# Probabilities times values in the first two mixers: from split operands to whole 32-bit operands, two heads in the column halves of the array

## The chip, the cores and the metric

One core of one Trainium2 chip runs the whole program once. The metric is the device time of that execution in microseconds (us). Engines are named as the profile names them: PE is TensorE's matrix multiply, PEld its weight load, DVE is VectorE, ACT is ScalarE, POOL is GpSimd, SP issues most of the DMAs.

## The reference

A residual stream of 512 tokens by 1024 features passes through two blocks, all in 32-bit floats. The first block has two layers, each a mixer and a squared-ReLU MLP; the mixers are the part that the change touches. A mixer holds 16 attention heads of width 64. In layer 0 these are 8 heads with a forget gate and 8 with a relative position bias; in layer 1 they are 8 heads of stick-breaking attention and 8 of latent attention (MLA). For every head the end is the same product over 512 queries and the keys that they may see:

```
p = softmax(scores + bias)            # or, in layer 1, the stick-breaking weights a
out = einsum('bhqk,bkhd->bqhd', p, v) # 64 values per head
...
x = x + concat(heads) @ w_out
x = x + squared_relu_mlp(rmsnorm(x), w_up, w_down)
```

The second block (differential attention, sparse attention, gates, SwiGLU) follows; the change does not edit its code.

## The kernel before, in words

Activations lie with features along the 128 partitions and the 512 tokens along the free axis. PE is fed with a short 32-bit format (fp32r in the rows). To keep the precision of whole 32-bit numbers each operand is split into two short parts, hi and lo, with hi + lo the number: ACT copies hi, DVE subtracts hi from the source to get lo (`split`), and products are sums of matmuls over the parts. Weight blocks are split in the same way as they arrive (`wr` raw, `wh` and `wl` the parts).

All instructions are first recorded by a `Recorder`, then issued engine by engine in the order of a list schedule (`schedule`), which uses planned durations (`cost`) and numbers of buffers (`BUFS`). So every instruction has the same line in the trace, L371, and rows are told apart by the names of their tiles.

A pair of heads t has heads u = 0 and 1. The steps that the change touches, for one head:

- `softmax` makes four probability tiles (names `x`), one per 128 queries, with the scores in `pss`; `turn` transposes them on PE (`psp<-cst,x`) into four tiles by keys j, `pt0` to `pt3`, 512, 384, 256 and 128 queries wide, and splits each: ACT writes hi (`pt<-psp`), DVE lo (`pt<-psp,pt`). In `stick_head` there is no transposition; an exponential in a tile `P` is masked and then split by POOL (hi, `pt<-P`) and DVE (lo, `pt<-P,pt`). Its first split, of another quantity, uses a `pt0` tile for j = 0 too.
- `v_tiles` makes the value tiles `V`, per head 64 columns hi beside 64 columns lo, with an ACT and a DVE instruction per 128 tokens.
- `av` multiplies. The stationary operand is the 128 columns (hi, lo) of V of one head, the moving one is hi, then lo of `pt`, so eight matmuls of all 128 columns of the array into the one buffer `pso`: rows 0:64 hold hi of V, rows 64:128 lo.
- `fold` adds the two halves of `pso` (ACT copies one to a `T` tile, DVE adds) into half u of a tile; `finish_pair` splits that tile for the output projection.

There are 16 pairs (32 heads, 8 of them stick-breaking). While PE waits for one head, the schedule puts matmuls of projections in between (`psg` and, in `fill`, parts of the output projection). Buffers: three `psg`, two `pss`, two `psp`, one `pso`; one tile of each `pt0` to `pt3`.

One more place matters, in the second block: `compress` multiplies whole 32-bit operands, with 62 stationary columns.

```
for l in range(16):
    ...
    nc.tensor.matmul(ps[0:62, 0:256], win[l // 8][:, l % 8].rearrange("p g c -> p (g c)"),
                     wt[:, 256 * (l % 2):256 * (l % 2) + 256], start=(l == 0), stop=(l == 15))
```

Its weight tile `wt` is named `rbcq` or `acc` in turn and serves two of the 16 matmuls; the stationary tile is `strip`.

Of the kernel before, what the change touches and what calls it, by code (L numbers as in the profile page):

```python
# [20 lines left out]
NT = 4  # L21
# [14 lines left out]
# --------------------------------------------------------------------------  # L36
# host side: layouts only
# --------------------------------------------------------------------------
class Packer:
    """Weights as one flat array of contiguous [128, width] blocks."""  # L40
# [12 lines left out]
    def stationary(self, key, w, cols=None):  # L53
        """[128 K, 128 M] pieces in the order (m, kt), eight to a block."""
# [31 lines left out]
class Columns:  # L86
    """Small [128, n] arrays side by side."""
# [161 lines left out]
class Recorder:  # L249
# [14 lines left out]
    def later(self, k):  # L264
        """what is recorded inside yields to the next k instructions, but for those that wait for it"""
# [4 lines left out]
    def flush(self):  # L270
        """all that is recorded so far comes first"""
# [49 lines left out]
    def cost(self, op):  # L321
# [7 lines left out]
        if e == "tensor":  # L329
# [3 lines left out]
            if op.args[2].dtype == F32:  # L333
                return max(4 * n / 2.4, 428)
# [19 lines left out]
    # from the end of one instruction to the start of a dependent one on another engine  # L354
# [26 lines left out]
    def sequence(self):  # L381
        """the instructions by priority: each before those that wait for it, what comes later in its own order"""
# [116 lines left out]
# --------------------------------------------------------------------------  # L499
# chip side  # L500
# --------------------------------------------------------------------------
class Net:
# [21 lines left out]
    def fetch(self, m, tag="x"):  # L524
        """residual tile m on chip"""
# [13 lines left out]
    def c(self, key):  # L539
# [4 lines left out]
            "sm": 16, "sm32": 3, "rbc": 1, "rbcq": 1, "strip": 2}  # L544
# [28 lines left out]
    def split(self, dst, src, scale=None):  # L573
        """dst[:, 0] + dst[:, 1] = src (* scale per partition), two short parts."""
# [19 lines left out]
    def gemm(self, key, mov, evac, tags="gggggggg", cols=slice(0, 512), kept=None):  # L594
        """out[m] = W[:, m]^T mov; evac(m, psum)."""
# [17 lines left out]
    def gemm_tok(self, key, stat, evac, blk=None):  # L613
        """out[token tile i] = stat^T W; evac(i, psum)."""
# [33 lines left out]
    def mean_cols(self, acc, n, eps=None):  # L648
        """[128 tokens, tiles] mean of squares (+ eps)."""
# [19 lines left out]
    def rows(self, col, outs):  # L669
        """[128, 512] with col[token] in every row; outs = [(tag, factor)]."""  # L670
# [12 lines left out]
    def prep(self, m, gain, spill=False, sq=0):  # L683
        """operand x*g of feature tile m and its share of the sum of squares."""
# [29 lines left out]
    def to_stack(self, ab):  # L714
        """per head [hi; lo]"""
# [8 lines left out]
    def to_dup(self, ab):  # L724
        """per head a tile (hi, lo) with its rows twice"""
# [18 lines left out]
    def softmax(self, i, passes, bias, gate=None):  # L744
        """P [128 q, keys] from negated scores, normalised."""
# [14 lines left out]
    def turn(self, ps_list):  # L760
        """four P tiles -> per key tile j [128 keys, (hi, lo), q]"""
        nc = self.nc
        res = []
        for j in range(NT):
# [4 lines left out]
            t = self.tl(f"pt{j}", [128, 2, w], F32R)  # L769
            self.split(t, pp[:, :w])  # L770
            res.append(t)
        return res

# [7 lines left out]
    def fold(self, o, dst, u):  # L781
        """O = rows 0:64 + rows 64:128, into half u of dst"""
# [5 lines left out]
    def v_tiles(self, key, stat, rcol, extra=None, blk=None):  # L788
        """value tiles [128 tokens, 4 heads, (hi, lo), 64]"""
# [3 lines left out]
        def evac(i, ps):  # L793
            t = self.tl("V", [128, 4, 2, 64], F32R)
# [24 lines left out]
    def soft_head(self, passes, bias, v, dst, u, gate=None):  # L819
        ps_list = [self.softmax(i, passes, bias, gate) for i in range(NT)]  # L820
        pt = self.turn(ps_list)
        o = self.psum("o")
        self.av(o, pt, v)
        self.fold(o, dst, u)
# [20 lines left out]
    def out_part(self, key, ops):  # L845
        """first part of an output projection, one residual tile at a time"""
# [14 lines left out]
    def even_mixer(self):  # L861
# [9 lines left out]
        vt = self.v_tiles("fox_v0", h, self.rcol, gates, self.first)  # L871
# [10 lines left out]
        # sums within a token tile, and of the tiles one, two and three before  # L882
# [32 lines left out]
        for kind, mk in (("fox", fox_bias), ("chk", chk_bias)):  # L915
            for t in range(4):
                if not (kind == "fox" and t == 0) and t % 2 == 0:
                    vt = self.v_tiles(f"{kind}_v{t // 2}", h, self.rcol)
# [16 lines left out]
    def odd_mixer(self):  # L935
# [10 lines left out]
        for t in range(4):  # L946
            if t % 2 == 0:
                vt = self.v_tiles(f"sb_v{t // 2}", h, self.rcol)
# [818 lines left out]
```

## Time and profile before

| What | Value |
|---|---|
| Median of 3 runs | 2093.58 us (2093.03 to 2095.36) |
| Profiled execution, span from first to last instruction | 2093.9 us |
| Mean granted TensorE clock of that execution | 0.991 |
| PE, PEld busy | 2038.8 us (97%), 1688.3 us (81%) |
| DVE, ACT, POOL busy | 1131.0, 896.5, 399.1 us (54%, 43%, 19%) |

The profiled execution is another one than the three timed; its span is 0.3 us above their median. Busy shares are means over a program with different stages; matmuls are pipelined, so that the busy time of PE contains overlaps, and the distance from the start of one matmul to the start of the next says more than the duration in its row. The first mixer runs from about 40 to 240 us of the span, the second from about 655 to 905 us; an MLP follows each, and the second block fills the time after some 1250 us.

### The profile page before, as it was taken

How to read it: one execution, taken by the hardware profiler on the slowest of the kernel's cores; microseconds unless marked ns; L12 is line 12 of the kernel's file. 1: busy time of each engine (PE TensorE's matmuls, PEld its weight loads, DVE VectorE, ACT ScalarE, POOL GpSimd, SP SyncE). 2: the span in 40 equal slices, each digit the busy share in tenths (PEclk: the TensorE clock that was granted, in tenths of full speed). 3: DMA queues.
4: the chain of work that ended last, by engine and by line, in shares of the span. 5: the costliest groups of instructions: out<-in, count | busy, mean ns of one | idle time of the engine just before them, and what ended most of it. 6: DMA issues, size and time to landing. Idle time of an engine off the chain costs nothing. (4 is left out here: it accounts for less than half of the span.)

```text
span 2093.9 us, 27228 instructions
## 1 busy us (share of the span) xinstructions
PE 2038.8 (97%) x9958; PEld 1688.3 (81%) x9958; DVE 1131.0 (54%) x2033; ACT 896.5 (43%) x1621; POOL 399.1 (19%) x524
## 2 busy tenths in 40 slices
PE   8999999999999999899999999989999999999998
PEld 7887878888888877778888888877788888888887
DVE  5657853443445666774434344766786644333334
ACT  5556542322335555643323243544685542222224
POOL 2343210000022453220000014212240221011013
PEclk9999999999999999999999999999999999999999
DMA  6445623323244415632333234474113222223222
GB/s 197 133 129 157 186 91 92 100 91 101 91 142 122 111 58 129 181 104 91 100 92 98 94 120 131 126 185 126 57 41 111 92 100 91 101 91 101 90 101 81
DMA packets 80294, 232.00 MB, mean 111 GB/s; under 512 B 11424, under 2 KB 15392, under 8 KB 80160
## 3 DMA queue, kind: packets, MB, share of 16 engines
q1 hardware_dynamic: 80160, 230.25, 35.9%
q8 instruction: 79, 1.29, 0.3%
q14 instruction: 55, 0.45, 0.1%
HBM read 183.04 MB, written 10.49 MB: 92 GB/s over the span
## 5 line engine op out<-in xcount | busy, mean ns | idle before, releaser
L371 PE MATMUL psg<-h,wh 128*128 128x512 f32 x2688 | 855.4, 396 | 0.9 <-ACT h L371 0.6
L371 ACT ACTIVATE wh<-wr 128x1024 fp32r<-128x1024 f32 (+3 forms) x313 | 326.6, 1043 | 864.3 <-PE psg L371 687.4
L371 PEld LDWEIGHTS psg<-h,wh 128*128 128x128 f32 x2688 | 504.3, 189 | 108.2 <-ACT h L371 1.4
L371 PE MATMUL psg<-h,wl 128*128 128x512 f32 x1344 | 532.5, 396 | 1.0 <-DVE wl L371 0.7
L371 DVE TENSOR_TENSOR wl<-wr,wh 128x1024 fp32r<-128x1024 f32 (+3 forms) x313 | 385.0, 1230 | 58.8 <-ACT wh L371 54.8
L371 PEld LDWEIGHTS psg<-h,wl 128*128 128x128 f32 x1344 | 253.9, 189 | 56.6 <-DVE wl L371 2.7
L371 PE MATMUL psg<-KK,wh 128*128 128x512 f32 (+1 forms) x788 | 240.6, 387 | 0.4 <-DVE V L371 0.2
L371 DVE TENSOR_TENSOR x<-psg,x 128x512 f32<-128x512 f32 (+1 forms) x120 | 78.2, 654 | 290.8 <-PE psg L371 290.7
L371 POOL TENSOR_TENSOR acc<-acc,T 128x512 f32<-128x512 f32 (+1 forms) x50 | 73.5, 1471 | 789.6 <-issue 639.5
L371 PE MATMUL psg<-V,wh 128*128 128x512 f32 (+1 forms) x672 | 207.9, 390 | 1.0 <-DVE G L371 1.0
L371 PEld LDWEIGHTS psg<-KK,wh 128*128 128x128 f32 x788 | 146.6, 188 | 32.2 <-ACT o L371 0.5
L371 PE MATMUL psg<-KK,wl 128*128 128x512 f32 (+1 forms) x394 | 151.7, 385 | 0.0
L371 PEld LDWEIGHTS psg<-V,wh 128*128 128x128 f32 x672 | 126.2, 189 | 29.0 <-ACT wh L371 1.1
L371 DVE SCALAR_TENSOR_TENSOR T<-psg,rbc 128x512 f32<-128x512 f32 x64 | 44.3, 692 | 174.9 <-PE psg L371 172.6
L371 PE MATMUL psg<-V,wl 128*128 128x512 f32 (+1 forms) x336 | 131.6, 392 | 0.0
L371 ACT ACTIVATE x<-x,sm 128x128 f32<-128x128 f32 (+1 forms) x192 | 106.6, 558 | 52.5 <-DVE sm L371 52.0
L371 PE MATMUL psg<-o,wh 128*128 128x512 f32 x384 | 127.7, 401 | 0.8 <-ACT wh L371 0.5
L371 PE MATMUL psg<-wh,h 128*128 128x256 f32 (+2 forms) x560 | 114.2, 291 | 6.7 <-ACT wh L371 6.7
L371 PE MATMUL pso<-pt,V 128*128 128x128 f32 (+3 forms) x432 | 108.0, 337 | 3.5 <-ACT pt L371 1.9
L371 POOL TENSOR_SCALAR x<-x,sm 128x128 f32<-128x128 f32 (+1 forms) x112 | 66.5, 599 | 173.2 <-DVE sm L371 121.0
L371 PEld LDWEIGHTS psg<-wh,h 128*128 128x128 f32 x560 | 92.0, 193 | 8.4 <-ACT wh L371 6.7
L371 POOL TENSOR_TENSOR T<-T,rbc 128x512 f32<-128x512 f32 x22 | 39.3, 1785 | 285.3 <-ACT T L371 285.3
(263 smaller groups left out, 2673.8 us busy)
## 6 DMA issues: line engine op xcount, KB each, us to landing
wr<-in_w_dram SPq DMA_DIRECT2D x302, 512.0 KB, 3.5
KK<-AB SPq DMA_DIRECT2D x48, 256.0 KB, 5.4
QS<-AB SPq DMA_DIRECT2D x48, 128.0 KB, 3.9
x<-xs SPq DMA_DIRECT2D x24, 256.0 KB, 3.3
xs<-P SPq DMA_DIRECT2D x16, 256.0 KB, 3.8
xs<-x SPq DMA_DIRECT2D x16, 256.0 KB, 2.0
h<-AB SPq DMA_DIRECT2D x16, 256.0 KB, 3.8
KK<-AB SPq DMA_DIRECT2D x32, 128.0 KB, 2.4
```

Of the source, the lines that this page charges most:

```text
L371: op.inst = getattr(getattr(nc, op.eng), op.name)(*op.args, **op.kw)
```

## The change

The product of probabilities and values takes whole 32-bit operands in the 16 pairs. P is copied once (ACT) or used as it comes from the exponential (stick-breaking), V is written once; the DVE and POOL instructions of these splits go. One pair's two heads write one `pso` tile: head 0 rows 0:64, head 1 rows 64:128, with a stationary operand of 64 columns each, and `av_two` issues the two heads' matmuls of each j one after the other. `fold` is not called in the mixers, and `finish_pair` splits `pso` itself. `pt0` to `pt3` get two buffers, of half the width in bytes. The planner's cost of a 32-bit matmul with 64 output rows becomes half of what it was for others. The second block keeps the split form (`turn`, `av`, `fold`), with its two parts in two tiles.

```diff
-                return max(4 * n / 2.4, 428)
+                return 2 * n / 2.4 if out.ap[0][1] == 64 else max(4 * n / 2.4, 428)
...
-            "sm": 16, "sm32": 3, "rbc": 1, "rbcq": 1, "strip": 2}
+            "sm": 16, "sm32": 3, "rbc": 1, "rbcq": 1, "strip": 2, "pt0": 2, "pt1": 2, "pt2": 2, "pt3": 2}
...
+    def turn_whole(self, ps_list):
...
+            t = self.tl(f"pt{j}", [128, w])
+            nc.scalar.activation(t, pp[:, :w], AF.Copy)
+            res.append(t)
+        return res
+
+    def av_two(self, pts, vt, u0):
...
+        o = self.psum("o")
+        for j in range(NT):
+            for u in range(2):
+                nc.tensor.matmul(o[64 * u:64 * u + 64, 128 * j:], vt[j][:, u0 + u], pts[u][j], start=(j == 0), stop=(j == NT - 1))
+        return self.finish_pair(o)
...
+            if whole:
+                t = self.tl("V", [128, 4, 64])
+                nc.scalar.activation(t, ps[:, 0:256].rearrange("p (h d) -> p h d", h=4), AF.Copy, scale=rcol[:, i:i + 1])
+                res.append(t)
...
-                ob = self.T()
+                pts = []
                 for u in range(2):
                     passes = [(qs[:, u], kk[u][:, 0]), (qs[:, u], kk[u][:, 1])]
-                    self.soft_head(passes, mk(2 * t + u), self.vhead(vt, 2 * (t % 2) + u), ob, u)
-                ops.append(self.finish_pair(ob))
+                    pts.append(self.soft_head(passes, mk(2 * t + u)))
+                ops.append(self.av_two(pts, vt, 2 * (t % 2)))
...
             if j == 0:
-                sp[0] = self.pair("pt0")
+                sp[0] = self.halves("P")
...
-            e = self.tl("P", [128, 512])[:, :w]
+            e = at[j] = self.tl(f"pt{j}", [128, w])
             nc.scalar.activation(e, y[:, :w], AF.Exp)
...
-            a_ = self.tl(f"pt{j}", [128, 2, w], F32R)
-            nc.gpsimd.tensor_scalar(a_[:, 0], e, 1.0, 1.0, ALU.mult, ALU.mult)
-            nc.vector.tensor_tensor(a_[:, 1], e, a_[:, 0].bitcast(F32), ALU.subtract)
-            at[j] = a_
-        o = self.psum("o")
-        self.av(o, at, v)
-        self.fold(o, dst, u)
```

The order on PE shows where the new matmuls stand. First PE's order before, in the first mixer, at the second head of the first pair (`psg` is a projection, `psp` a transposition, `pso` the product; the last number is the width):

```order
L371 MATMUL pso_195<-pt_116_188,V_111 128x512
L371 MATMUL psg_285<-h_95,wh_287 128x512 x2
L371 MATMUL psg_285<-h_95,wl_288 128x512
L371 MATMUL psp_191<-cst,x_180 128x128
L371 MATMUL psp_191<-cst,x_184 128x128
L371 MATMUL pso_195<-pt_116_188,V_111 128x512
L371 MATMUL psp_193<-cst,x_184 128x128
L371 MATMUL pso_195<-pt_118_190,V_113 128x384 x2
L371 MATMUL psg_285<-h_97,wh_287 128x512
L371 MATMUL pso_195<-pt_120_192,V_115 128x256
```

Every row fills all 128 columns of the array; the products of one head are strewn among transpositions and projections. Now PE's order after the change, at the same pair: first the place of head 0's widest product, some 50 rows ahead of the rest.

```order
L371 MATMUL psp_162<-cst,x_151 128x128
L371 MATMUL psp_162<-cst,x_155 128x128
L371 MATMUL pso_192<-pt_87_159,V_111 64x512
L371 MATMUL psp_164<-cst,x_155 128x128
L371 MATMUL psg_269<-wl_268,h_95 128x256
```

This product of 64 columns stands alone between matmuls of 128 columns. Then the rest of the pair on PE, after the change:

```order
L371 MATMUL psp_188<-cst,x_181 128x128
L371 MATMUL pso_192<-pt_113_185,V_111 64x512
L371 MATMUL psp_190<-cst,x_181 128x128
L371 MATMUL pso_192<-pt_89_161,V_113 64x384
L371 MATMUL pso_192<-pt_115_187,V_113 64x384
L371 MATMUL pso_192<-pt_91_163,V_115 64x256
L371 MATMUL pso_192<-pt_117_189,V_115 64x256
L371 MATMUL pso_192<-pt_93_165,V_117 64x128
L371 MATMUL pss_223<-KK_207,QS_206 128x512
L371 MATMUL pso_192<-pt_119_191,V_117 64x128
L371 MATMUL pss_223<-KK_207,QS_206 128x512
```

Head 1's widest product has moved behind head 1's transpositions and stands alone as well; only the narrower ones stand head beside head, and here the last is cut off by a score matmul. Over the 16 pairs there are 44 such unbroken stretches of 64-column products on PE: 11 pairs have two lone 512-wide products and a stretch of six (broken once more in two of them), the 4 stick-breaking pairs have one lone product and a stretch of seven, as in the next piece, and the last pair of the first mixer has one stretch of eight. In the second mixer, at the first stick-breaking pair, PE's order after the change:

```order
L371 MATMUL psg_1260<-wl_1255,h_1093 128x256
L371 MATMUL pso_1191<-pt_1118_1190,V_1129 64x512
L371 MATMUL pso_1191<-pt_1092_1164,V_1131 64x384
L371 MATMUL pso_1191<-pt_1112_1184,V_1131 64x384
L371 MATMUL pso_1191<-pt_1088_1160,V_1133 64x256
L371 MATMUL pso_1191<-pt_1108_1180,V_1133 64x256
L371 MATMUL pso_1191<-pt_1084_1156,V_1135 64x128
L371 MATMUL pso_1191<-pt_1104_1176,V_1135 64x128
L371 MATMUL psg_1260<-wh_1254,h_1093 128x256
```

Head 0's 512-wide product stands 40 rows ahead of it, between a score matmul and another accumulation of 128 columns.

## Rows read from the trace of the kernel before

**Rows 1.** The page: span, busy time of each engine.

```profile
span 2093.9 us, 27228 instructions
...
PE 2038.8 (97%) x9958; PEld 1688.3 (81%) x9958; DVE 1131.0 (54%) x2033; ACT 896.5 (43%) x1621; POOL 399.1 (19%) x524
```

**Rows 2.** Busy time of each engine in the stretches of the two mixers.

```profile
40.00:240.00 200.00, 194.91 (x1146) 166.32 (x1145) 133.13 (x348) 114.58 (x271) 73.21 (x140) 1.00 0.57 157
655.00:905.00 250.00, 232.51 (x1251) 194.93 (x1252) 176.47 (x365) 145.12 (x325) 98.68 (x176) 0.99 0.43 120
```

**Rows 3.** What PE waited for from 40 to 905 us: total, times, longest.

```profile
PE psp L371 <- POOL pt L371: 2.4, 3, 1.2
...
PE pso L371 <- ACT pt L371: 1.3, 2, 0.6
...
PE pso L371 <- POOL pt L371: 0.5, 1, 0.5
...
PE psp L371 <- DVE pt L371: 0.4, 2, 0.2
PE pso L371 <- DVE T L371: 0.3, 1, 0.3
```

**Rows 4.** PE's timeline at one stick-breaking head: start, length, instructions merged.

```profile
684.20 0.40 PE L371 MATMUL pso<-pt,V 128*128 128x512 f32 x1
684.43 0.33 PE L371 MATMUL psp<-X,vcmp 128*128 128x128 f32 x2
...
685.12 1.16 PE L371 MATMUL pso<-pt,V 128*128 128x512 f32 x7
686.11 0.80 PE L371 MATMUL pss<-KK,QS 128*128 128x256 f32 x4
```

**Rows 5.** PE's timeline at eight matmul records of `compress`.

```profile
1433.76 0.64 PE L371 MATMUL psg<-h,wh 128*128 128x512 f32 x2
1434.33 1.08 PE L371 MATMUL psg<-rbcq,strip 128*62 128x256 f32 x4
1435.24 1.03 PE L371 MATMUL psg<-acc,strip 128*62 128x256 f32 x4
1436.20 0.50 PE L371 MATMUL psg<-h,wl 128*128 128x512 f32 x1
1436.53 0.63 PE L371 MATMUL psg<-h,wh 128*128 128x512 f32 x2
1437.00 0.39 PE L371 MATMUL psg<-h,wl 128*128 128x512 f32 x1
```

**Rows 6.** PE's timeline at two matmul records of `compress`.

```profile
1426.97 0.64 PE L371 MATMUL psg<-acc,strip 128*62 128x256 f32 x2
1427.54 0.73 PE L371 MATMUL psg<-h,wh 128*128 128x512 f32 x2
```

**Rows 7.** Timeline of weight loads and matmuls in another run of `compress`.

```profile
1389.11 0.62 PEld L371 LDWEIGHTS psg<-rbcq,strip 128*62 128x62 f32 x4 [1.73 <-DVE strip L371]
1389.11 1.08 PE L371 MATMUL psg<-rbcq,strip 128*62 128x256 f32 x4 [1.29 <-DVE strip L371]
...
1389.81 0.78 PEld L371 LDWEIGHTS psg<-acc,strip 128*62 128x62 f32 x4
```

**Rows 8.** DVE from 40 to 905 us: groups by tile, busy, mean ns.

```profile
L371 DVE TENSOR_TENSOR pt<-psp,pt 128x512 fp32r<-128x512 f32 (+1 forms) x96 | 43.2, 484 | 15.5 <-ACT pt L371 15.0
...
L371 DVE TENSOR_TENSOR T<-pso,T 64x512 f32<-64x512 f32 x32 | 21.8, 682 | 16.5 <-ACT T L371 16.3
...
L371 DVE TENSOR_TENSOR pt<-P,pt 128x128 fp32r<-128x128 f32 (+3 forms) x32 | 18.3, 585 | 10.2 <-POOL pt L371 10.1
...
L371 DVE SCALAR_TENSOR_TENSOR V<-psg,sm,V 128x256 fp32r<-128x256 f32 x28 | 13.3, 479 | 6.0 <-ACT V L371 5.9
```

**Rows 9.** The same view of ACT.

```profile
L371 ACT ACTIVATE T<-pso 64x512 f32<-64x512 f32 x32 | 19.1, 596 | 28.6 <-PE pso L371 28.3
```

**Rows 10.** The same view of POOL.

```profile
L371 POOL TENSOR_SCALAR pt<-P 128x128 fp32r<-128x128 f32 (+3 forms) x32 | 17.5, 555 | 1.4 <-PE pso L371 0.7
```

More of the change, by code (lines that the diff above doesn't have):

```diff
@@ L768, in turn @@
                 nc.tensor.transpose(pp[:, 128 * (i - j):128 * (i - j) + 128], ps_list[i][:, 128 * j:128 * j + 128], self.c("ident"))
-            t = self.tl(f"pt{j}", [128, 2, w], F32R)
+            t = Two(self.tl(f"pt{j}", [128, w], F32R), self.tl(f"pt{j}", [128, w], F32R))
             self.split(t, pp[:, :w])
@@ L772, in turn @@
         return res
+    def turn_whole(self, ps_list):
+        nc = self.nc
+        res = []
+        for j in range(NT):
+            w = 512 - 128 * j
+            pp = self.psum("p")
+            for i in range(j, NT):
+                nc.tensor.transpose(pp[:, 128 * (i - j):128 * (i - j) + 128], ps_list[i][:, 128 * j:128 * j + 128], self.c("ident"))
+            t = self.tl(f"pt{j}", [128, w])
[3 more added lines that the diff above has]
+    def av_two(self, pts, vt, u0):
+        nc = self.nc
+        o = self.psum("o")
+        for j in range(NT):
+            for u in range(2):
+                nc.tensor.matmul(o[64 * u:64 * u + 64, 128 * j:], vt[j][:, u0 + u], pts[u][j], start=(j == 0), stop=(j == NT - 1))
+        return self.finish_pair(o)
     def av(self, o, pt, v, start=True, stop=True):
@@ L786, in fold, with v_tiles @@
         nc.vector.tensor_tensor(dst[64 * u:64 * u + 64], o[0:64], t[0:64], ALU.add)
-    def v_tiles(self, key, stat, rcol, extra=None, blk=None):
+    def v_tiles(self, key, stat, rcol, extra=None, blk=None, whole=False):
         nc = self.nc
@@ L793, in evac @@
         def evac(i, ps):
+            if whole:
+                t = self.tl("V", [128, 4, 64])
+                nc.scalar.activation(t, ps[:, 0:256].rearrange("p (h d) -> p h d", h=4), AF.Copy, scale=rcol[:, i:i + 1])
+                res.append(t)
+                if extra is not None:
+                    extra(i, ps)
+                return
             t = self.tl("V", [128, 4, 2, 64], F32R)
@@ L817, in qk, with soft_head @@
         return res
-    def soft_head(self, passes, bias, v, dst, u, gate=None):
-        ps_list = [self.softmax(i, passes, bias, gate) for i in range(NT)]
-        pt = self.turn(ps_list)
-        o = self.psum("o")
-        self.av(o, pt, v)
-        self.fold(o, dst, u)
+    def soft_head(self, passes, bias):
+        return self.turn_whole([self.softmax(i, passes, bias) for i in range(NT)])
     def finish_pair(self, t):
@@ L869, in gates @@
                                            ALU.mult, ALU.add)
-        vt = self.v_tiles("fox_v0", h, self.rcol, gates, self.first)
+        vt = self.v_tiles("fox_v0", h, self.rcol, gates, self.first, whole=True)
         e = self.small(32)
@@ L917, in even_mixer @@
                 if not (kind == "fox" and t == 0) and t % 2 == 0:
-                    vt = self.v_tiles(f"{kind}_v{t // 2}", h, self.rcol)
+                    vt = self.v_tiles(f"{kind}_v{t // 2}", h, self.rcol, whole=True)
                 q, k = self.qk(f"{kind}_qk{t}", h, rbcq, rbc, "op" if kind == "fox" and t == 0 else "gg")
@@ L947, in odd_mixer @@
             if t % 2 == 0:
-                vt = self.v_tiles(f"sb_v{t // 2}", h, self.rcol)
+                vt = self.v_tiles(f"sb_v{t // 2}", h, self.rcol, whole=True)
             q, k = self.qk(f"sb_qk{t}", h, rbcq, rbc)
@@ L951, in odd_mixer @@
             qd = self.to_dup(q)
-            ob = self.T()
-            for u in range(2):
-                self.stick_head(ks[:, u], qd[u], self.vhead(vt, 2 * (t % 2) + u), ob, u, ntri, nones)
-            ops.append(self.finish_pair(ob))
+            pts = [self.stick_head(ks[:, u], qd[u], ntri, nones) for u in range(2)]
+            ops.append(self.av_two(pts, vt, 2 * (t % 2)))
         C, S = self.cs
@@ L991, in odd_mixer @@
         self.fill(half, OUT1[0], 0)
-        vt = self.v_tiles("ukv_v0", ckv, rkv)
+        vt = self.v_tiles("ukv_v0", ckv, rkv, whole=True)
         rqb, = self.rows(rq, [("rbcq", -(96.0 ** -0.5))])
@@ L1015, in odd_mixer @@
             if t == 2:
-                vt = self.v_tiles("ukv_v1", ckv, rkv)
+                vt = self.v_tiles("ukv_v1", ckv, rkv, whole=True)
             q = qkd(f"uq_nope{t}", cq, rqb)
             k = qkd(f"ukv_k{t}", ckv, rkb)
-            ob = self.T()
+            pts = []
             for u in range(2):
@@ L1069, in stick_head @@
                                     channel_multiplier=-1)
[L1070 to L1076 removed]
+        return at
     def sincos(self, pos, freq, tag="strip"):
```

8 lines of the change are left out of this document (3 added, 5 removed).

## The prediction

> **What bounds the kernel now.** I read the page first: PE is busy 97% of the span, DVE 54%, ACT 43% and POOL 19% [rows 1]. Then the same by stretch, for the two mixers alone: there PE is idle 5.1 us of 200 and 17.5 us of 250, 22.6 us together, while DVE, the next busiest, works two thirds of the time [rows 2]. Third, what PE waited for in these stages [rows 3]: no single wait exceeds some microseconds, and only few are waits for the instructions that the change takes out. So each mixer is bound by PE's stream of matmuls; a microsecond more on PE is a microsecond more in the end unless it falls into the 22.6 us of idle time, and work taken from DVE, ACT or POOL pays only through that idle time. The last views are timelines of PE, in which I read the distance from start to start, since the durations overlap.
>
> **What the change removes.** From DVE the lo parts of P (43.2 us after transpositions, 18.3 us in stick-breaking), the folds (21.8 us) and the lo parts of V (13.3 us) [rows 8]; from ACT the folds' copies, 19.1 us [rows 9]; from POOL the hi parts in stick-breaking, 17.5 us [rows 10]. That is 96.6 us of DVE's work. It was hidden behind PE, except where PE waited for it. The waits that surely lose their cause are those on the hi and lo parts and the folds: 0.5 + 0.4 + 0.3 = 1.2 us [rows 3]. The upper bound is all of PE's idle time in both stretches, 22.6 us [rows 2]. I take 4.9 us: the 1.2 us, and the two other waits for operands named pt, 2.4 us on POOL and 1.3 us on ACT, whose instructions stay but stand in shorter queues [rows 3]. What remains late is the ACT copy of the transposed P and, in MLA, transfers of queries and keys, which the change leaves alone.
>
> **What the products cost before.** A clean stretch shows one head: the first 512-wide product from 684.20 to 684.43 us, the other seven from 685.12 to 686.11 us, so 0.23 + 0.99 = 1.22 us [rows 4]. 32 heads: 39.0 us of PE.
>
> **What they cost after.** No row has a 64-column product of this kind; the nearest are the 62-column matmuls of whole 32-bit operands in `compress`. There each of the two matmuls of a weight tile has become two records, four per tile. Eight records last 1.87 us from the first start to the start of the next matmul [rows 5], two last 0.57 us [rows 6]; six more records cost 1.30 us, 0.217 us each for 256 columns. So a 256-wide whole matmul costs 0.434 us, although it uses half of the array. In proportion, a record of 512, 384, 256 and 128 columns takes 0.434, 0.325, 0.217 and 0.108 us, and a matmul is two of them. The planner's 2n/2.4 for one matmul is half of that: it is right only if the other half of the array works at the same time.
>
> If the halves never overlap, a pair costs 4 x (0.434 + 0.325 + 0.217 + 0.108) = 4.34 us, and 16 pairs 69.4 us: 30.3 us more than before. If they overlap, what matters is the order. A lone 512-wide product has no partner: 0.868 us. In a stretch, records start in their order, and two records of one half follow each other; so the second record of head 0 can lie beside the first of head 1, but not the first records beside each other. For the six products of 384, 384, 256, 256, 128 and 128 columns the starts are 0 and 0.325, 0.325 and 0.65, 0.65 and 0.867, 0.975 and 1.192, 1.192 and 1.300, 1.409 and 1.517, and the end is 1.63 us instead of 2.60. Counted alike, the stretch of seven takes 2.17 us and that of eight 2.60 us. The order after the change has 11 pairs with two lone products and a six, 4 with one lone product and a seven, one eight: 11 x (1.74 + 1.63) + 4 x (0.87 + 2.17) + 2.6 = 51.8 us, 12.7 us more than before. No row tells which of the two holds, since every 62-column matmul of the trace lies in the same half. I take the overlap: the halves hold different weights and write different rows of PSUM, and nothing in the rows makes the one need what the other uses.
>
> **What entering and leaving costs.** Around those eight records lie plain 512-wide matmuls, whose pace is (1437.00 - 1436.53) / 2 = 0.235 us. The two before the visit take 0.57 us instead of 0.47, the one behind it 0.33 instead of 0.235 [rows 5]; and in the visit of two records 0.57 - 2 x 0.217 = 0.14 us go beyond the records' own pace [rows 6]. So one visit to the 62-column form costs 0.10 + 0.14 + 0.10 = 0.34 us: matmuls of the full width and of the narrow one do not follow each other without a gap. The old products had the full width and could be strewn anywhere for nothing. The new order has 44 visits: 44 x 0.34 = 15.0 us. Lower bound: where PE waits for the operand anyway the entry is hidden, 0.24 us each, 10.6 us. I take the full price, for few of these places had a wait [rows 3]. Weight loads add nothing: in the narrow form too the next tile's loads start at 1389.81 us, while the matmuls that began at 1389.11 run until 1390.19 [rows 7].
>
> [...]
>
> **The smaller edits.** The output's split reads `pso` instead of a T tile, with the same two instructions; the one `pso` buffer was held through a fold, now through this split, both of an ACT and a DVE instruction. The copies of P and V on ACT stay as long as they were. Two half-size buffers of each pt hold a pair; the next pair's first copies wait for this pair's products, as the next head's did before. I put all of this at nothing: it lies behind projections that PE has at hand. If that cover is gone, one such wait is of the size of those in the list, 0.3 to 2.4 us [rows 3].
>
> **The sum.** +12.7 for the products, +15.0 for the visits, -4.9 for waits: +22.8 us. The profiled span is 2093.9 us [rows 1], 0.3 us above the median of the runs, 2093.6; the forecast is 2116.4 us.
>
> **The rivals.**
>
> Halves in turn. The second half starts only when the first has finished. For it speaks that no row shows two matmuls side by side; against it, only that nothing visible forbids it. It gives 30.3 + 15.0 - 4.9 = +40.4, 2134.0 us.
>
> [...]
>
> Freed engines fill PE's idle time. The place is the odd mixer, where POOL and DVE feed PE in turns and PE idles 17.5 us [rows 2]; relieved of 96.6, 19.1 and 17.5 us of work they would arrive early everywhere. At its full 22.6 us, with entries hidden, the sum is 12.7 + 10.6 - 22.6 = +0.7, 2094.3 us: no change. It decides once the relief exceeds 23.3 us, which takes shorter waits in the second block too, whose order shifts with the planner's clock. Against it: of the listed waits on pt and the folds only 4.9 us can be tied to the removed work [rows 3].
>
> The change frees nothing and costs nothing (the DVE work was hidden, the products cost the same) would need the planner's price and free visits; the rows of `compress` contradict both.
>
> **How the numbers follow.** Forecast 0.57, its own range +12.0 (12.7 + 10.6 and half of the idle time gone, 11.3) to +26.5 (27.7 - 1.2): 2105.6 to 2120.1. Halves in turn 0.25, from 30.3 + 10.6 - 11.3 to 30.3 + 15.0 - 1.2, 2123 to 2138. The freed engines 0.13, of it 0.08 within 0.2% and 0.05 faster. The weight-load rule 0.03, above the range; 0.02 for a luckier order elsewhere, faster. A measurement of this kernel can tell 0.2%, 4.2 us, from no change. So faster 0.07, same 0.08, slower 0.85; the range 2099 to 2138 leaves out most of the third rival and the 0.03 above.
>
> **What would show it.** In the trace after, the 64-column records should have 0.43 us per 512 columns, 256 of them. Right: in a stretch of eight, a head's second record starts together with the other head's first, and the whole lasts 2.6 us; wrong, if it lasts 4.3. At lone products the neighbours' starts should show some 0.34 us beyond the pace. DVE's busy time in the mixers falls by some 97 us with PE's idle time hardly changed. The forecast fails if PE's idle time falls by more than 10 us, or if visits between 64 and 128 columns cost nothing.

## The result, and the profile after

The changed kernel takes 2103.6 us (median of 14 runs, 2100.28 to 2112.97) against 2093.85 us for the kernel before (14 runs beside them): ratio 1.0052 [1.0038, 1.0067], that is +10.9 us (8.0 to 14.0). It became slower, as forecast, and lies in the range, but by a little less than half of the 22.8 us. The clock has no part in it that shows: the mean granted clock is 0.9928 over these runs and 0.9930 over the 72 runs of the kernel before that stood beside the experiments (those beside the result have no clock on record).

The page after, first lines:

```profile
span 2100.6 us, 26862 instructions
...
PE 2048.6 (98%) x9958; PEld 1668.7 (79%) x9958; DVE 1044.1 (50%) x1841; ACT 879.3 (42%) x1589; POOL 368.8 (18%) x492
```

Busy time by engine in the windows of [rows 2] (PE, PEld, DVE, ACT, POOL):

```profile
40.00:240.00 200.00, 194.09 (x1091) 151.61 (x1090) 91.09 (x252) 101.52 (x243) 66.00 (x138) 1.00 0.53 141
655.00:905.00 250.00, 235.54 (x1234) 184.44 (x1234) 128.01 (x267) 134.10 (x305) 71.62 (x142) 0.98 0.45 125
```

DVE lost 90.5 us in them (133.1 + 176.5 before), about as forecast; PE's idle time in these rows went only from 22.6 to 20.4 us. What PE waited for from 40 to 905 us, the view of [rows 3]:

```profile
PE pss L371 <- DMA KK<-AB: 3.6, 3, 1.3
PE pss L371 <- DMA QS<-AB: 3.4, 1, 3.4
PE pss L371 <- issue: 3.4, 4, 1.7
PE pss L371 <- POOL acc L371: 2.6, 1, 2.6
...
PE psp L371 <- POOL x L371: 1.1, 3, 0.4
PE pso L371 <- DVE o L371: 0.9, 1, 0.9
```

No wait for `pt` or `T` is left among the large ones; a new one on `pso` is for its own split (`o`). Now PE's timeline at a softmax pair in the first mixer, with a lone product (one that has no 64-column product as a neighbour) at 62.27 us, a stretch (an unbroken row of 64-column products) at 63.53 us, and then the one stretch of eight, x16 because each product is two records:

```profile
61.96 0.38 PE L371 MATMUL psp<-cst,x 128*128 128x128 f32 x2
62.27 1.07 PE L371 MATMUL pso<-pt,V 128*64 128x512 f32 x2
63.27 0.33 PE L371 MATMUL psp<-cst,x 128*128 128x128 f32 x1
63.53 1.51 PE L371 MATMUL pso<-pt,V 128*64 128x384 f32 x10
64.97 0.50 PE L371 MATMUL pss<-KK,QS 128*128 128x512 f32 x1
...
246.56 0.63 PE L371 MATMUL psg<-o,wh 128*128 128x512 f32 x2
247.11 2.37 PE L371 MATMUL pso<-pt,V 128*64 128x512 f32 x16
249.42 0.50 PE L371 MATMUL psg<-o,wl 128*128 128x512 f32 x1
249.76 0.64 PE L371 MATMUL psg<-o,wh 128*128 128x512 f32 x2
```

A lone product lasts 1.00 us from start to next start, 2 x 0.434 + 0.13: a half of the array that works alone takes the full time of its two records. The stretch of eight lasts 249.42 - 247.11 = 2.31 us. One half's records need 2.17, and 0.14 is the visit's own share as in `compress`; the forecast was 2.60 + 0.14. So both halves work all the time. The view of windows for `pso` alone shows how (count of records in flight in brackets):

```profile
247.10:247.20 0.10, 0.09 (x2) 1.00 0.80 328
```

Two records stand there within 0.1 us, and the trace has their starts 6 ns apart, 247.112 and 247.118 us; the next two follow at 247.592 and 247.598 us. Each head's first record lies beside the other's first, not beside its second.

To see where the rest went I summed PE's distances from start to start in three parts, which add up to the time between PE's first and last matmul. This is worked out from the trace: "work" is every matmul at the pace of its kind (the 30th percentile of its form, width and neighbours in the same kernel), with the 64-column products at their whole distance; "beyond" is what goes beyond that pace at a granted clock of 1.00; "half" is the same in stretches with the granted clock at 0.50, in which the pace is half (in the changed kernel from 731.72 to 735.13 us one 512-wide matmul starts every 0.43 us instead of every 0.23). Layer 0's mixer runs to the start of its MLP, layer 1's likewise. About 15 us ahead of PE's first matmul and behind its last are left out. The border between work and beyond depends on what is taken as a kind and where a stage begins: another choice shifts the parts by one to three microseconds.

```
us of PE               layer 0's mixer      layer 1's mixer      the rest
                       work beyond half     work beyond half     work  beyond half
before                231.4  17.5  0.0     249.8  40.6  3.5     1477.0  48.8  10.3
before, second time   231.4  17.6  0.0     249.7  40.1  1.9     1477.7  48.4   7.2
changed               243.0  16.2  0.0     260.3  31.5  4.5     1478.3  47.3   4.6
eight together        231.8  15.3  0.0     249.8  31.3  8.4     1478.3  48.5   5.0
eight, by twos        232.2  14.8  0.0     250.2  31.1  6.5     1478.4  46.5  10.4
eight, head by head   244.2  15.6  0.0     262.2  27.2  7.1     1478.5  47.9   5.0
two and six           233.9  17.3  1.6     251.0  29.8  7.1     1478.4  48.4   4.9
layer 1's mixer alone 231.4  18.9  0.0     261.3  28.4  3.9     1478.5  46.5   4.7
layer 0's mixer alone 243.2  15.8  0.0     249.8  39.4  3.7     1477.4  49.2   6.3
before without lo     230.5  21.4  0.0     249.7  35.1  1.8     1478.2  46.4  10.6
eight + lo, idle      232.0  16.0  0.0     251.3  38.2  7.0     1479.5  45.5   7.9
eight + split, idle   231.8  17.4  0.0     249.8  37.8  5.1     1478.8  46.6   4.6
```

From before to changed, PE's work in the two mixers rises by 11.6 + 10.5 = 22.1 us, and what goes beyond it falls by 1.3 + 9.1 = 10.4 us, nearly all in layer 1's mixer. The rest gives back 0.2. That is +11.5 us, inside the interval of the measured +10.9. The half-clock parts are left out: they fall by 4.7 us from before to changed (13.8 to 9.1), which is why the two profiled spans differ by only 6.7 us (2093.9 and 2100.6), but they differ as much between two executions of the same program (the first two lines of the table).

### The profile page after: what moved, and what is told of

Read it like the earlier page. It is cut to its first block, busy times and chain, and to the rows that moved or that the text cites. A ratio compares the mean times of both kernels' runs of the same rounds, so it can differ in the third digit from the quotient of the medians.

```text
span 2100.6 us, 26862 instructions
## 1 busy us (share of the span) xinstructions
PE 2048.6 (98%) x9958; PEld 1668.7 (79%) x9958; DVE 1044.1 (50%) x1841; ACT 879.3 (42%) x1589; POOL 368.8 (18%) x492
## 5 line engine op out<-in xcount | busy, mean ns | idle before, releaser
L371 ACT ACTIVATE pt<-psp 128x512 f32<-128x512 f32 (+3 forms) x208 | 84.1, 435 | 59.0 <-PE psp L371 55.9
L371 PE MATMUL pso<-pt,V 128*64 128x384 f32 (+7 forms) x432 | 102.2, 403 | 2.5 <-DVE o L371 0.9
L371 POOL TENSOR_SCALAR x<-x,sm 128x128 f32<-128x128 f32 (+1 forms) x112 | 61.2, 553 | 209.2 <-DVE sm L371 181.5
```

What stands on the lines that cost most here:

```text
L371: op.inst = getattr(getattr(nc, op.eng), op.name)(*op.args, **op.kw)
```

## The experiments

The theory after the result: the extra cost lies only in the order (lone products and visits; a visit is one change to 64 columns and back), and the relief of the other engines, PE's time that comes back because they have less to do, is about 10 us. The rivals: the halves are still partly in turn; or there is little relief, and the cost was small.

**Eight together.** All eight products of a pair are one unit of the schedule, in the order of the change, so 16 visits without a lone product.

```diff
+        grp = []
         for j in range(NT):
             for u in range(2):
-                nc.tensor.matmul(o[64 * u:64 * u + 64, 128 * j:], vt[j][:, u0 + u], pts[u][j], start=(j == 0), stop=(j == NT - 1))
+                grp.append(nc.tensor.matmul(o[64 * u:64 * u + 64, 128 * j:], vt[j][:, u0 + u], pts[u][j], start=(j == 0), stop=(j == NT - 1)))
+        self.rec.fused.append(grp)
...
+            grp[0].deps = grp[0].deps | alld
+            for a, b in zip(grp, grp[1:]):
+                b.deps = b.deps | {a.n}
...
+            for op in grp[1:]:
+                op.prio = -1
```

The first product waits for what all eight need (`alld`), the others follow it at once.

> All eight products of a pair are issued as one unbroken stretch, 16 stretches instead of 44; nothing else is edited. Theory (each half of the array works through its own records, whatever stands between in the other half; a lone product costs its full 0.868 us; a visit costs some 0.30 us): the products' own records fall from 47.9 us, as the trace after shows them, to 16 x 2.17 = 34.7 us, and 28 visits less save 8.4 us; with up to 4 us of new waits, because the first product of a pair comes later, about 18 us less than the changed kernel: near 2086 us, some 8 us below the kernel before. Rival (the lone products stood where PE would have waited anyway, so their price was hidden): within 4 us of the changed kernel, 2100 to 2107 us.

Measured: 2086.22 us (8 runs), ratio to the kernel before 0.9953 [0.9933, 0.9972], faster than both kernels and as expected. One stretch on PE's timeline:

```profile
76.14 0.63 PE L372 MATMUL psg<-h,wh 128*128 128x512 f32 x2
76.70 2.37 PE L372 MATMUL pso<-pt,V 128*64 128x512 f32 x16
79.01 0.50 PE L372 MATMUL psg<-h,wl 128*128 128x512 f32 x1
79.35 0.64 PE L372 MATMUL psg<-h,wh 128*128 128x512 f32 x2
```

2.31 us again. The neighbours give the visit: 76.70 - 76.14 = 0.56 instead of 0.47, 0.14 inside, 79.35 - 79.01 = 0.34 instead of 0.235, together 0.34 us, the price that the prediction took from `compress`. By the table the mixers' work is back at that of before (231.8 and 249.8), so all that is left is relief: beyond falls by 2.2 + 9.3 = 11.5 us. A count without the table agrees: 16 x (2.17 + 0.34) = 40.2 us for products and visits, 1.2 more than the 39.0 before, and the kernel is 9.9 us faster by its ratio, so some 11 us came back elsewhere. The delay of waiting for all operands of a pair hardly shows.

**Eight, head by head.** The same unit, but head 0's four products first (the edit against eight together).

```diff
-        for j in range(NT):
-            for u in range(2):
+        for u in range(2):
+            for j in range(NT):
```

> The same unbroken stretch of eight, but ordered head by head: head 0's four products, then head 1's four. Theory (two halves with a queue each): head 1's records start beside head 0's although four products stand ahead of them; a stretch still lasts about 2.2 us and the time is that of the other order within 3 us, near 2086 us. Rival (only products that are neighbours in the order overlap; starts keep the order otherwise): only head 0's last record lies beside head 1's first, a stretch lasts about 4.2 us, 16 x 2 = 32 us more, near 2118 us.

Measured: 2105.09 us (9 runs), ratio 1.0047 [1.0028, 1.0066]. The same place, and the windows view for `pso`:

```profile
76.79 0.62 PE L372 MATMUL psg<-h,wh 128*128 128x512 f32 x2
77.35 3.93 PE L372 MATMUL pso<-pt,V 128*64 128x512 f32 x16
81.21 0.50 PE L372 MATMUL psg<-h,wl 128*128 128x512 f32 x1
```

```profile
77.35:77.60 0.25, 0.25 (x1) 1.00 0.00 0
78.85:78.95 0.10, 0.10 (x3) 1.00 0.12 41
```

3.86 us, neither 2.31 (free overlap) nor 4.48 (in turn). At first one record is in flight. Starts in the trace: head 0's 512, 512, 384, 384 at 77.349, 77.829, 78.258, 78.581, its first 256-wide record at 78.903, and head 1's first 512-wide one at 78.909. So head 1 begins together with head 0's fifth record, ahead of the sixth to eighth, which stand before it in the program. Its first record is the ninth of the program and starts with the fifth: a lead of four records. With that lead only 2 x 0.217 + 2 x 0.108 = 0.65 us are shared: 4.34 - 0.65 + 0.14 = 3.83. Both the theory and its rival missed this reach.

**Eight, by twos.** If the reach is four records, two products of one head may stand together for nothing (the edit against eight together).

```diff
-        for j in range(NT):
-            for u in range(2):
+        for j, u in ((0, 0), (1, 0), (0, 1), (1, 1), (2, 0), (3, 0), (2, 1), (3, 1)):
```

> The stretch of eight ordered by twos: two products of head 0, two of head 1, and so on. Head by head, head 1's first record started together with the record four places ahead of it, and not earlier. Theory (a record can start when the one four places ahead of it starts, if its own half is free): full overlap here, a stretch of 2.3 us, the time of the stretch of eight within 3 us. Rival (overlap only with the neighbouring product): the stretch lasts 0.6 us longer or more, 10 us in all.

Measured: 2086.97 us (6 runs), ratio 0.995 [0.9931, 0.9968], as for eight together, and the work in the table agrees within 0.4 us for each mixer. The stretch at 76.48 us lasts 2.36 us to the next start (78.84), 0.05 more than for eight together. So four records of one half ahead of the other half cost next to nothing here, while head by head, with eight ahead, head 1 started with the fifth. Four records are two products; the runs do not tell which of the two is counted.

**Two and six.** The two 512-wide products are one unit, the six others another: 27 visits, no lone product (the edit against eight together).

```diff
-        self.rec.fused.append(grp)
+        self.rec.fused += [grp[:2], grp[2:]]
```

> Two units per pair, the two 512-wide products and the six narrower ones; 27 stretches in the order instead of 16, no lone product. Theory: the records cost the same 34.7 us as in one stretch of eight, and 11 more visits cost 0.30 us each: 3 us more than the stretch of eight, near 2089 us. If visits and not lone products made most of the changed kernel's extra time, at 44 visits against 27, this run would lie about 13 us above the stretch of eight.

Measured: 2088.1 us (8 runs), ratio 0.9959 [0.9943, 0.9974]. Eleven visits more than eight together cost 2.1 + 1.2 = 3.3 us of work in the table, 0.30 us each; the medians differ by 1.9 us. So of the changed kernel's 22.1 us of work its 28 visits more than eight together make some 8.4. The larger part, some 13 us, is lone products: by the bare records the changed order takes 47.8 us and stretches of eight 16 x 2.17 = 34.7.

**The removed work put back, idle (two attempts).** To eight together I added the removed hi and lo parts, copies and folds as instructions whose results nobody reads, first into `T` tiles (the edit below, without V's lo parts), then, for DVE's results, into a scratch tile `scr` of one byte per element.

```diff
+            nc.vector.tensor_tensor(self.T()[:, :w], pp[:, :w], t, ALU.subtract)
...
+        for u in range(2):
+            f = self.T()
+            nc.scalar.activation(f[0:64], o[64:128], AF.Copy)
+            nc.vector.tensor_tensor(self.T()[0:64], o[0:64], f[0:64], ALU.add)
...
+            f, g = self.T()[:, :w], self.T()[:, :w]
+            nc.gpsimd.tensor_scalar(f, e, 1.0, 1.0, ALU.mult, ALU.mult)
+            nc.vector.tensor_tensor(g, e, f, ALU.subtract)
```

> The stretch of eight with the removed work of the other engines put back as dead work: DVE subtracts the copy of P and of V from their sources, ACT and DVE do the folds, POOL and DVE the split in stick-breaking, into tiles that nobody reads. The number of stretches on PE stays 16. Theory (the freed engines gave back some 10 us of PE's waits, twice what the forecast put in): 7 to 11 us slower than the stretch of eight without it, near 2094 us, with these microseconds in PE's waits in the mixers. Rival (the waits hardly depend on this work, the smaller loss was luck with the clock): within 3 us of the stretch of eight.

> The stretch of eight again with the removed work put back as dead work, now with DVE's results in a scratch tile of one byte an element that nothing else uses, since the first try let them queue for three tiles that other work needs. Theory (the freed engines give back about 10 us of PE's waits): 6 to 11 us slower than the stretch of eight, 2092 to 2097 us. Rival (the waits hardly depend on it): within 3 us of 2086 us.

Measured: 2205.26 us, ratio 1.0518 [1.0492, 1.0544], and 2178.15 us, ratio 1.0398 [1.0376, 1.0421]. Both failed as tests of the relief. PE's waits in the first mixer of the second attempt, and then PE's busy time and granted clock by ten microseconds:

```profile
PE psg L372 <- DVE scr L372: 12.8, 3, 4.3
PE psp L372 <- DVE scr L372: 7.1, 9, 1.4
PE pss L372 <- ACT T L372: 6.9, 4, 3.0
```

```profile
60.00:70.00 10.00, 5.94 (x38) 0.90 0.02 5
70.00:80.00 10.00, 8.83 (x31) 0.50 0.00 0
...
90.00:100.00 10.00, 6.57 (x30) 0.66 0.05 3
100.00:110.00 10.00, 10.00 (x45) 1.00 0.56 170
```

PE waits longest for idle results and `T` copies. The timelines of ACT and DVE before a wait of 4.3 us for `scr`, which ends at 93.43 us, show why:

```profile
89.24 1.08 ACT L372 ACTIVATE T<-pso 64x512 f32<-64x512 f32 x2 [3.66 <-PE pso L372]
91.07 0.60 ACT L372 ACTIVATE o<-pso 128x512 fp32r<-128x512 f32 x1 [0.75 <-DVE scr L372]
91.56 0.59 ACT L372 ACTIVATE T<-pss 128x512 f32<-128x512 f32 x1
```

```profile
92.91 1.51 DVE L372 SCALAR_TENSOR_TENSOR scr<-psg,sm,V 128x256 uint8<-128x256 f32 x3
```

The two idle folds of a pair (`T<-pso`) wait for the end of PE's stretch, the split of `pso` (`o<-pso`) waits for them, and behind both stands what PE's buffers wait for: on ACT the copy of scores (`T<-pss`), on DVE the idle lo parts of V (`scr<-psg`), for which PE waited here. PE starves, and the granted clock is low in the same stretch: 0.90 in the row from 60 us, 0.50 in that from 70 us, and 1.00 again in that from 100 us, with PE busy throughout. In the second attempt some 60 us beyond pace lie in stretches at 0.50 (my sum, as in the table), against 13.8 in the kernel before. That prices a longer chain, not a longer queue.

**Before without lo parts.** The kernel before without DVE's lo parts of P; the matmuls stay.

```diff
-            self.split(t, pp[:, :w])
+            if self.lo:
+                self.split(t, pp[:, :w])
+            else:
+                nc.scalar.activation(t[:, 0], pp[:, :w], AF.Copy)
...
-                nc.tensor.matmul(o[:, 128 * j:], v(j), pt[j][:, a], start=(start and j == 0 and a == 0),
+                nc.tensor.matmul(o[:, 128 * j:], v(j), pt[j][:, a if self.lo else 0], start=(start and j == 0 and a == 0),
...
-            nc.vector.tensor_tensor(a_[:, 1], e, a_[:, 0].bitcast(F32), ALU.subtract)
```

> The kernel before, with the lo parts of P in the first two mixers left out: DVE's subtractions are gone (61.5 us of DVE's 96.6 us), and the second product of each tile takes hi once more, so that the values are not those of the reference and PE does the same matmuls as before. It shows the relief alone, without narrow products. Theory: DVE lets go of the transposed tiles in PSUM sooner and PE's waits fall by 5 to 8 us, near 2088 us. Rival (the waits lie elsewhere): within 2 us of the kernel before.

Measured: 2092.06 us (12 runs), ratio 0.9983 [0.9973, 0.9992], about -3.6 us, less than the 5 to 8 expected. Beyond falls by 5.5 in layer 1's mixer and rises by 3.9 in layer 0's. So 61.5 us of DVE's work [rows 8] alone buy about a third of the relief.

**Layer 1's mixer alone, layer 0's mixer alone.** In each, one mixer has the change and the other the old form (the edit of layer 1 alone):

```diff
-                    vt = self.v_tiles(f"{kind}_v{t // 2}", h, self.rcol, whole=True)
+                    vt = self.v_tiles(f"{kind}_v{t // 2}", h, self.rcol)
...
-                ops.append(self.av_two(pts, vt, 2 * (t % 2)))
...
+                    self.av(o, pt, self.vhead(vt, 2 * (t % 2) + u))
+                    self.fold(o, ob, u)
+                ops.append(self.finish_pair(ob))
```

> The change in the odd mixer alone; the even mixer keeps split operands and folds. In the traces the even mixer grew by 10.3 us, the odd one by 2.4 us in its three stages, and the rest shrank by stretches of lower clock. Theory: the loss is the even mixer's, so this kernel lies 0 to 4 us above the kernel before. Rival (the loss is spread over all 16 pairs alike): half of the whole loss, 5 us above it, or more.

> The change in the even mixer alone, with its lone products; the odd mixer as before. The odd mixer alone came out 0.2% below the kernel before. Theory (the parts add: in the even mixer PE hardly waited, so nothing pays for narrow products and visits; the odd one pays for its own): 11 to 16 us above the kernel before, more than the whole change. Rival (the parts do not add, the order of the whole decides): within 3 us of the changed kernel or below it.

Measured: layer 1's mixer alone 2091.87 us (11 runs), ratio 0.9981 [0.9967, 0.9995]; layer 0's alone 2101.18 us (9 runs), ratio 1.0027 [1.001, 1.0043]. Both expectations missed: layer 1 alone came out some 4 us below the kernel before, where 0 to 4 us above it was expected, and layer 0 alone 5.7 us above it, where it was 11 to 16; this is where its rival had it, within 3 us of the changed kernel. The table splits it: layer 1's pays 11.5 us of work and gets 12.2 back; layer 0's pays 11.8 and gets 1.7 back. PE's waits from 655 to 905 us with the change in layer 1 alone, the first rows:

```profile
PE pss L371 <- DMA xs<-P: 2.6, 1, 2.6
PE pss L371 <- DMA QS<-AB: 1.6, 1, 1.6
PE psg L371 <- DVE G L371: 1.5, 2, 1.2
```

The two transfers and `G` cost about what they cost before (2.6, 1.7 and 1.0 us in this window); the waits on `pt` are gone. The two ratios sum to +0.8 thousandths where the whole change has +5.2 [3.8, 6.7]; the parts of the table nearly add up (23.3 of work, 13.9 of relief, against 22.1 and 10.4). The difference lies in the relief, which shifts by some microseconds from one schedule to another. Every edit here also changes the order that the schedule plans, and no run separates that order from the freed engines; this stays open.

**Parts of the removed work put back, idle.** Eight together with DVE's lo parts of the transposed P only, and eight together with POOL's and DVE's split in stick-breaking only, both into scratch, without folds.

```diff
+            nc.vector.tensor_tensor(self.tl("scr", [128, 512], mybir.dt.uint8)[:, :w], pp[:, :w], t, ALU.subtract)
```

```diff
+            f = self.T()[:, :w]
+            nc.gpsimd.tensor_scalar(f, e, 1.0, 1.0, ALU.mult, ALU.mult)
+            nc.vector.tensor_tensor(self.tl("scr", [128, 512], mybir.dt.uint8)[:, :w], e, f, ALU.subtract)
```

> The stretch of eight with one dead part put back: DVE subtracts the copy of the transposed P from its source in PSUM, 64 + 32 times, into a scratch tile; no folds, nothing in stick-breaking. The folds put back had lengthened the chain on the one pso buffer, so that those two runs measured something else. Theory: DVE's lo parts held PE up by 2 to 5 us through the transposed tiles in PSUM, near 2090 us. Rival: within 1.5 us of the stretch of eight.

> The stretch of eight with the split in stick-breaking put back as dead work, 32 instructions on POOL and 32 on DVE. PE's waits in that stage fell by 4 to 6 us with the change. Theory (the queues of POOL and DVE made these waits): 3 to 6 us slower than the stretch of eight, and its stage of stick-breaking longer by as much. Rival (the waits went because the product's operand no longer passes through two engines, not because of the queues): within 1.5 us.

Measured: 2092.92 us (12 runs), ratio 0.9992 [0.998, 1.0005], 6.7 us above eight together by the medians; and 2089.8 us (12 runs), ratio 0.998 [0.9967, 0.9994], 3.6 us above it. These runs and those of eight together stood beside different runs of the kernel before; by the ratios the two differences are 8.2 and 5.7 us. For the lo parts 2 to 5 us were expected, for stick-breaking 3 to 6. PE's waits in the MLA stage with the idle lo parts (795 to 922 us):

```profile
PE psg L372 <- DVE wl L372: 2.2, 2, 1.2
PE psp L372 <- DVE scr L372: 2.0, 3, 1.1
...
PE pss L372 <- POOL acc L372: 1.4, 1, 1.4
PE psg L372 <- ACT wh L372: 1.3, 2, 0.8
```

and in the same stage of eight together (793 to 914 us):

```profile
PE psg L372 <- DVE wl L372: 1.0, 1, 1.0
...
PE psg L372 <- ACT wh L372: 0.5, 1, 0.5
...
PE pss L372 <- POOL acc L372: 0.3, 1, 0.3
```

The stage goes from 120.7 to 126.6 us. Only 2.0 us of it wait for the idle instructions themselves; the weight splits (`wl`, `wh`) and `acc`, which nobody changed, come later by 1.2, 0.8 and 1.1 us. `wl` stands in DVE's queue, as the idle instructions do; `wh` is ACT's and `acc` POOL's, whose queues got nothing here, so these two are late by way of other instructions, and which is not shown. The split in stick-breaking lengthens that stage from 150.9 to 156.5 us, with POOL's busy time at 64.80 us instead of 45.97 (first eight together, then with the idle split):

```profile
624.10:775.00 150.90, 144.02 (x804) 120.70 (x804) 68.96 (x109) 81.11 (x171) 45.97 (x101) 0.97 0.37 101
626.30:782.80 156.50, 146.82 (x805) 118.47 (x804) 86.23 (x141) 79.56 (x171) 64.80 (x133) 0.98 0.36 97
```

Together the two cost 10.3 us by the medians and 13.9 by the ratios, at least as much as eight together gains on the kernel before (9.9 us by its ratio), with some microseconds of uncertainty on each. So putting back a part of the removed work undoes the gain, and its size agrees roughly with what taking away gave. The parts do not add up, though: the lo parts of P cost 6.7 to 8.2 us when those of the transposed P alone are put back, and gave 3.6 when all were taken from the kernel before. The share of the folds and of V's lo parts stays open as well, since the folds could not be put back without the harm above.

**The kernel before once more**, to see whether two sets of runs of one program agree.

> The kernel before, unchanged, for the granted clock of its single runs, which is known for the changed kernel (mean 0.9928 of 14 runs, 0.990 to 0.996) and only for the one profiled execution of before (0.991). If PE's fewer waits in the changed kernel also lower the time at half clock, the mean here lies below 0.992. Rival: the two kernels have the same mean within 0.0005, and the 4.7 us at half clock by which the two profiled executions differ are chance. The time is that of before, 2090 to 2103 us.

Measured: 2092.24 us (10 runs), ratio 0.9996 [0.9982, 1.001]; mean clock 0.9936 against 0.9929 over the 32 runs of the same program beside it. The theory (below 0.992) is wrong, and 0.9928 for the changed kernel differs by a little more than the rival's 0.0005. Means of the clock differ by some 0.0007 between sets of the same program, so the nearly equal means of before and after exclude no more than that; across those 32 runs 0.001 less clock goes with 1.9 us more time, so the clock is at most some 1.3 us of the 10.9.

## Why the prediction was half right

The direction and its reason held: PE's stream is the bound, and the new order makes it longer. The size was double, and its three terms were all wrong to the same side, so nothing cancelled. Point by point:

- **What the products cost after.** That the halves overlap was right, though the prediction had no row for it, and the rival of the halves in turn is out. The step "the second record of head 0 can lie beside the first of head 1, but not the first records beside each other" failed. It was my estimate: [rows 5] shows records in their order within one half, and no row showed it across two. With both halves working through their own records, a six takes 1.30, a seven 2.17, an eight 2.17 us (worked out; with the 0.14 inside a visit the trace after has 1.44 us for the ten records from 63.53 us, 2.29 for the seven at 690.55 and 2.31 for the eight at 247.11): 11 x 3.04 + 4 x 3.04 + 2.17 = 47.8 us instead of 51.8. The term is +8.8 instead of +12.7.
- **Entering and leaving.** 44 visits were there, and 0.34 us is exact beside 512-wide matmuls. Among transpositions visits share a part: at 62.27 us the entry costs 0.09 (0.31 for two transpositions, whose pace is 0.11), the inside 0.13, and the one transposition between this product and the next stretch takes 0.26 instead of 0.11, which is the exit of one visit and the entry of the next at once. The mean is 0.30 (22.1 - 8.8 over 44), as in two and six: +13.3 instead of +15.0.
- **The relief of the other engines.** This step failed most: "I take 4.9 us: the 1.2 us, and the two other waits for operands named pt". It was 10.4 us. Two readings were wrong. First, PE's idle time in [rows 2] was taken as all that could be won; since the durations in PE's rows overlap the next start (the lone product at 62.27 us lasts 1.07 us, the next matmul starts after 1.00), a late start can hide in it. In the same two windows the distances beyond pace were some 50 us before and 40 after (my sum, as in the table), while the idle time went from 22.6 to 20.4. Second, only waits for the folds and for operands named `pt` were counted; the idle lo parts put back made PE wait longer for others (`wl`, `wh`, `acc`) as well. By what path the freed engines gave back each microsecond stays open.
- **The sum.** 8.8 + 13.3 - 10.4 - 0.2 (the rest) = +11.5 against the forecast's +22.8: of the 11.3 us between them the relief is 5.5, the overlap 3.9, the visits 1.7.
- **The rivals.** The freed engines did fill PE's time in the mixer that the prediction named, the odd one (layer 1's), but to 9.1 us, not 22.6, and the other mixer got almost nothing. The weight-load rule, 0.03 of the chances, is shown by no run: in the stretch of eight at 247.11 us the 16 records have 16 loads, 0.13 to 0.14 us each, and in one half they follow each other at their bare pace, 0.21 to 0.22 us for 256 columns. Column halves side by side gain: 2.31 us measured, where the two halves in turn would take 4.48 (worked out: 4.34 + 0.14).
- **What was to show it.** DVE's busy time fell by 90.5 us in the two windows, near the 97 named. "The forecast fails if PE's idle time falls by more than 10 us" named the right quantity; it has to be read from starts.

## What to carry to other kernels

When matmuls go from the full array to halves of it, keep both halves' products in one unbroken group, in an order that feeds both halves. Here a lone 512-wide product took 1.00 us (at 62.27 us, changed kernel) and two side by side 1.01 us (two and six, 61.70 to 62.71 us), a visit cost 0.30 us in the mean (0.34 between 512-wide matmuls), and the grouping alone turned +0.5% into -0.5%. When an edit takes work off busy engines, count not only the waits for that work but also the instructions that come later because of it, and measure PE's lost time from start to start, not from busy time. A test that puts work back must not lengthen a chain on a single buffer.

## What the runs showed of the hardware

- Column halves run apart. In the stretch of eight of the changed kernel, records in different halves start 6 to 7 ns after each other (247.112 and 247.118 us), and a half's record may start ahead of earlier ones of the other half. Head by head, head 1's first, the ninth of the program, starts at 78.909 us, with head 0's fifth (78.903) and ahead of its sixth (79.119). In the changed kernel's stretch of seven at 690.55 us, head 0's last, the twelfth, starts at 691.790 us, with head 1's sixth of the program (691.779) and ahead of its ninth (692.101).
- A visit from 128 to 64 columns and back costs 0.34 us between 512-wide matmuls: in eight together 0.56 us instead of 0.47 ahead of it, 0.14 inside and 0.34 instead of 0.235 behind it.
- The granted clock was halved during a wait of PE. In the changed kernel PE waits 3.4 us for `QS`, until 730.69 us (PE's busy time and granted clock around it):

```profile
724.00:730.00 6.00, 3.25 (x15) 0.96 0.91 223
730.00:736.40 6.40, 5.71 (x16) 0.51 0.84 199
736.40:742.00 5.60, 5.60 (x33) 1.00 0.00 1
```

PE is busy 3.25 of 6 us. Within that row the granted clock is 1.00 until 729.4 us and 0.50 from 729.6 us (0.96 in the mean), ahead of the end of the wait. It stays at 0.50 for nearly the whole of the next 6.4 us (0.51) and is 1.00 in the row after that, with PE busy throughout. What sets it is not shown.
